# The first weights of a channel mixer split by adding DMAs, and a gate's conditioning moved to the mixer's front

## The chip, the cores and the metric

The kernel runs on one core of one Trainium2 chip. The metric is the device time of one execution in microseconds (us). TensorE (PE in the rows) multiplies, VectorE (DVE), ScalarE (ACT) and GpSimd (POOL) work elementwise, and SyncE (SP) issues most DMAs. Each engine runs its own queue strictly in order.

## The reference

One layer of a streaming encoder, float32, 512 tokens of width 1024, one sequence. A conditioning vector c gives six vectors of width 1024: a shift, a scale and a gate for each of the two sub-layers. The first is a token mixer (attention and a state-space branch, merged and projected). The second is the channel mixer, about which the change is:

```python
c_act = jax.nn.silu(c)
mod = c_act @ w_ada[l] + b_ada[l]
sh_m, sc_m, g_m, sh_f, sc_f, g_f = [m[:, None, :] for m in jnp.split(mod, N_MOD, axis=-1)]
...
x = _layer_norm(DEEPNORM_ALPHA * x + (1.0 + g_m) * y, ln1_g[l], ln1_b[l])
h = _normalize(x) * (1.0 + sc_f) + sh_f
gate, up = jnp.split(h @ w_ffn_in, 2, axis=-1)        # 1024 -> 2 x 2816
y = (jax.nn.silu(gate) * up) @ w_ffn_out              # 2816 -> 1024
x = _layer_norm(DEEPNORM_ALPHA * x + (1.0 + g_f) * y, ln2_g[l], ln2_b[l])
```

`g_f`, the last gate, is wanted only in the last line.

## The kernel before

**Products.** A float32 operand x is split in two rounded parts, `hi` (a copy in the type float32r) and `lo = x - hi`, and a product is three matmuls: hi·hi, hi·lo and lo·hi (`mm3`). So each weight tile costs a load into `raw` (512 KB, 8 buffers), a copy on ACT into `whi` (4 buffers) and a lower part in `wlo` (4 buffers). Before the change the lower part is made in one of two ways. `sub` subtracts on DVE or POOL. With `eng=None` (in `unit`, for the attention's weights) ACT writes -raw rounded, which is -hi, into `wlo`, and POOL issues a DMA that adds `raw` to it: an *adding DMA*.

**Tiles in a pool and slots.** Scratch tiles of 512 columns are 53 slots (`s0` to `s52` in the rows), taken by `get()` and given back by `put()`; the eight PSUM banks are `b0` to `b7`. A buffer is reused only when its last reader is done, so a load into a used buffer waits in SP's queue, and all loads behind it too, since `load` keeps the program's order on SP.

**Order.** A scheduler sets the order of the instructions on each engine from priorities (`prio`). The loads keep the order of the code.

**The stage around the change.** The token mixer ends with the projection `proj` (weights `w_out`), then `ln1_block` runs for each of four blocks of 128 tokens: gate, add, two layer norms, transposes through PSUM (L967), scale and shift (L972, L974), and the split of the modulated activations into the tiles `h0` (high, L978) and `h1` (low, L159 on DVE). The channel mixer then needs both. It begins with four weight units of `w_ffn_in` (two in `raw` buffers as whole units, two in slots by `slot_unit`); `first_half(0)` multiplies them with the first 256 tokens. Two further products for the first two pairs of column tiles, `p_x1` and `p_b`, come next, then `first_half(256)`, and then the loop `for dp in range(ND)` over ten pairs (seven products each, with sums of weights and of activations, which saves multiplications).

**The last gate.** `ada_gate_pe` makes a quarter of g_f: it clears 256 columns on POOL, loads a row of the bias and 8 x 128 x 256 of `w_ada` (two `raw` buffers, called `ra`), multiplies by the conditioning vector on PE (eight narrow matmuls, plain float32, which the trace counts as 16) and adds on DVE (L272). Before, the four quarters stand in the loop at dp 2 to 5. At dp 6 two matmuls with a matrix of ones spread the gate over all partitions (L1168). The tiles are those of the first gate, `gmx`.

Of the kernel before, what the change touches and what calls it, by code (L numbers as in the profile page):

```python
# [17 lines left out]
ALU = mybir.AluOpType  # L18
# [40 lines left out]

ENG, FENG = "VGVVVGVGGGGVVGGG", "GGGV"  # L60

# [20 lines left out]
def _build(tc, I, out):  # L82
# [75 lines left out]
    def sub(dst, a, b, eng=V):  # L158
        return eng.tensor_tensor(dst, a, b, ALU.subtract)  # L159

    def split(x, n=512, eng=V, keep=False):

        h, l = get(F32R), get(F32R)
        acopy(h[:, :n], x[:, :n])  # L164
        sub(l[:, :n], x[:, :n], h[:, :n], eng)
        if not keep:
            put(x)
        return h, l

    def unit(view, a, b, eng=V):  # L170


        with prio("feed"):
            raw = wp.tile([P, D], F32, tag="raw", name=nm("raw"), bufs=NRAW)
            load(raw.rearrange("p (a b) -> p a b", a=a), view)
            hi = wp.tile([P, D], F32R, tag="whi", name=nm("whi"), bufs=NHI)
            lo = wp.tile([P, D], F32R, tag="wlo", name=nm("wlo"), bufs=NHI)
            acopy(hi, raw)  # L178
            if eng is None:
                act(lo, raw, AF.Copy, scale=-1.0)  # L180
                G.dma_start(out=lo, in_=raw, accum_op=ALU.add)
            else:
                sub(lo, raw, hi, eng)
        return hi.rearrange("p (a b) -> p a b", a=a), lo.rearrange("p (a b) -> p a b", a=a)
# [718 lines left out]
    with prio("mix"):  # L903
# [92 lines left out]
        for i in range(NT):  # L996
            with prio("first"):
                ln1_block(i)
        put(*l1g, *l1b)


    with prio("ffn"):
        first, wx = [], []
        for i in range(FIRST):
            for c in (0, FH):
                view = w_f[:, :, c + P * i:c + P * i + P]
                if len(first) < 2:
                    w = unit(view, KC, P, (V, G)[FENG[len(first)] == "G"])
                    w = [[x[:, k, :] for x in w] for k in range(KC)]
                else:  # L1010
                    pair = slot_unit(view, KC, P, (V, G)[FENG[len(first)] == "G"])
                    wx += pair
                    w = [[x[:, k % 4 * P:k % 4 * P + P] for x in pair[k // 4]] for k in range(KC)]
                first.append(w)
# [34 lines left out]

        def operand(x):  # L1050
            with prio("feed"):
                hi = wp.tile([P, D], F32R, tag="whi", name=nm("whi"), bufs=NHI)
                lo = wp.tile([P, D], F32R, tag="wlo", name=nm("wlo"), bufs=NHI)
                acopy(hi, x)  # L1054
                sub(lo, x, hi)
            return hi, lo

        def product(o, x, h, first):
            w = operand(x)
            for q in range(2):  # L1060
# [42 lines left out]
        def p_x1(dp):  # L1103
            d = dps[dp]
            d["a"], d["c"] = piece(dp, 0, 0), None
            d["X"], d["c1"] = bk.get(), get()
            product(d["X"], d["a"], half(0, 0), True)
            acopy(d["c1"], d["X"])

        def p_b(dp):  # L1110
            d = dps[dp]
            d["b"] = piece(dp, 0, 4)
            o = bk.get()
            product(o, d["b"], half(4, 0), True)
            tt(d["c1"], o, d["c1"], ALU.add)
            bk.put(o)
            silu(d["c1"])

        first_half(0)
        for dp in range(2):  # L1120
# [7 lines left out]
        acts, spent = [], []  # L1128
        gfx = gmx
        for g in part:  # L1130
# [3 lines left out]
        for dp in range(ND):  # L1134
# [26 lines left out]
            d["f"] = d["c1"], v  # L1161
            if 2 <= dp < 6:
                j = dp - 2
                ada_gate_pe(5, j, gfx[j // 2][:, j % 2 * 256:j % 2 * 256 + 256])
            if dp == 6:
                for j in range(2):
                    p_ = bk.get()
                    mm(p_, ones, gfx[j], True, True)  # L1168
                    act(gfx[j], p_, AF.Identity, bias=one_c)
                    bk.put(p_)  # L1170
        put(*held)
# [121 lines left out]
```

## Time and profile before

| | us |
|---|---|
| time, median of 3 runs | 824.61 (824.35 to 826.85) |
| profiled execution, its own time | 824.6 |
| its span | 822.9 |
| PE busy in the span | 758.1 (92%) |
| DVE busy | 586.4 (71%) |
| ACT busy | 438.8 (53%) |
| POOL busy | 148.4 (18%) |

The span is the time from the first to the last instruction on the core. A busy share is an average over stages that have different limits, so it is read stage by stage below.

### The profile page before, as it was taken

The page shows a single profiled execution, that of the slowest core. Times are in us where ns is not written, and L with a number is a line of the kernel's source. Part 1 is how long each engine was busy: PE and PEld are TensorE (multiplying, and loading weights), DVE is VectorE, ACT ScalarE, POOL GpSimd, SP SyncE. Part 2 cuts the span into 40 slices and gives each one's busy share as a digit, 9 for nine tenths or more (in the row PEclk, how much of TensorE's full clock was granted, in tenths as well). Part 3 has the DMA queues.
Part 4 walks back from the last instruction along what each step waited for, and adds up shares of the span by engine and source line. Part 5 has one row for each costly group of instructions (what it writes and reads, how often), then busy time and mean ns, then how long its engine had stood idle before and what let it go on. Part 6 is the DMA issues. An engine that isn't in the chain of part 4 may idle for free.

```text
span 822.9 us, 12321 instructions
## 1 busy us (share of the span) xinstructions
PE 758.1 (92%) x4767; PEld 667.5 (81%) x4767; DVE 586.4 (71%) x975; ACT 438.8 (53%) x715; POOL 148.4 (18%) x161
## 2 busy tenths in 40 slices
PE   4989989999996797999994999999999999999995
PEld 2878879988885676787883989999999999888884
DVE  5798474884658774878799898777787876434267
ACT  4375644678987676761435473534445456532211
POOL 1443244512323221001634000000000000000013
PEclk9999998999997999899998899999999999999998
DMA  9992227964207792925941004414445344440001
GB/s 281 361 242 67 52 64 153 237 137 77 52 10 196 228 232 92 350 70 187 358 120 52 1 19 136 155 53 146 144 143 183 104 139 145 157 148 27 1 26 76
DMA packets 99498, 111.49 MB, mean 135 GB/s; under 512 B 4456, under 2 KB 86384, under 8 KB 99440
## 3 DMA queue, kind: packets, MB, share of 16 engines
q1 hardware_dynamic: 95552, 96.82, 37.1%
q0 software_dynamic: 3744, 13.63, 9.0%
q8 instruction: 37, 0.61, 0.3%
q10 hardware_dynamic: 144, 0.26, 0.1%
q14 instruction: 21, 0.17, 0.1%
HBM read 94.97 MB, written 2.10 MB: 118 GB/s over the span
## 4 chain that ended last, share of the span: by engine, by line
PE 75%; DVE 10%; DMA 6%; issue 3%; ACT 2%; SPq 2%; POOL 1%; POOLq 0%; DVEq 0%; ACTq 0%
PE b L149 74%; DMA ra<-w_ada 3%; SPq L146 2%; DMA s<-w_in 1%; DVE s L252 1%; DVE st L288 1%; DMA raw<-w_glu 1%; DMA wlo<-raw 1%; DVE h L159 1%; DVE s L407 1%; DMA s<-x 0%; DVE s L159 0%; DVE s L972 0%; DVE s L943 0%; DVE s L477 0%
## 5 line engine op out<-in xcount | busy, mean ns | idle before, releaser
L149 PE MATMUL b<-h,whi 128*128 128x256 f32 (+1 forms) x896 | 216.5, 331 | 20.8 <-DVE h L159 9.4
L149 PEld LDWEIGHTS b<-h,whi 128*128 128x128 f32 x896 | 151.5, 191 | 36.5 <-DVE h L159 9.6
L159 DVE TENSOR_TENSOR wlo<-raw,whi 128x1024 fp32r<-128x1024 f32 x103 | 129.6, 1264 | 72.1 <-ACT whi L178 37.1
L149 PE MATMUL b<-s,whi 128*128 128x256 f32 (+1 forms) x800 | 168.5, 308 | 7.6 <-ACT whi L178 6.8
L149 PE MATMUL b<-h,wlo 128*128 128x256 f32 (+1 forms) x448 | 148.2, 331 | 1.4 <-DMA wlo<-raw 1.4
L149 PEld LDWEIGHTS b<-s,whi 128*128 128x128 f32 x800 | 129.7, 190 | 18.0 <-ACT whi L178 6.9
L149 PE MATMUL b<-whi,s 128*128 128x512 f32 (+1 forms) x392 | 122.6, 390 | 0.0
L149 PE MATMUL b<-s,wlo 128*128 128x256 f32 (+1 forms) x400 | 121.5, 306 | 0.0
L159 DVE TENSOR_TENSOR s<-s,s 128x512 fp32r<-128x512 f32 (+4 forms) x112 | 76.4, 689 | 56.4 <-PE b L149 23.0
L178 ACT CAST whi<-raw 128x1024 fp32r<-128x1024 f32 x66 | 69.0, 1048 | 84.7 <-PE b L149 66.5
L1054 ACT CAST whi<-raw 128x1024 fp32r<-128x1024 f32 x70 | 72.7, 1050 | 77.5 <-PE b L149 41.6
L149 PEld LDWEIGHTS b<-h,wlo 128*128 128x128 f32 x448 | 85.8, 192 | 8.9 <-DMA wlo<-raw 1.9
L149 PEld LDWEIGHTS b<-whi,s 128*128 128x128 f32 x392 | 73.2, 188 | 16.6
L149 PE MATMUL b<-s,s 128*128 128x128 f32 (+2 forms) x438 | 81.9, 317 | 2.0 <-POOL s L159 1.4
L164 ACT CAST s<-s 128x512 fp32r<-128x512 f32 (+1 forms) x106 | 57.7, 569 | 41.3 <-DMA s<-w_in 12.1
L149 PEld LDWEIGHTS b<-s,wlo 128*128 128x128 f32 x400 | 75.7, 190 | 3.7
L149 PEld LDWEIGHTS b<-s,s 128*128 128x128 f32 x438 | 68.5, 192 | 11.2 <-POOL s L159 1.6
L149 PE MATMUL b<-wlo,s 128*128 128x512 f32 (+1 forms) x196 | 76.4, 390 | 0.0
L1233 POOL TENSOR_TENSOR s<-s,s 128x512 f32<-128x512 f32 x6 | 8.5, 1430 | 357.1 <-DVE s L1232 357.1
L159 POOL TENSOR_TENSOR s<-s,s 128x512 fp32r<-128x512 f32 (+1 forms) x32 | 40.2, 1264 | 79.0 <-ACT s L164 77.6
L1047 DVE TENSOR_TENSOR raw<-raw,raw 128x1024 f32<-128x1024 f32 x40 | 48.6, 1219 | 4.8 <-DMA raw<-w_ffn_in 4.3
L252 DVE SCALAR_TENSOR_TENSOR s<-ra,ca,s 128x256 f32<-128x256 f32 x88 | 47.2, 557 | 4.0 <-DMA ra<-w_ada 3.2
(246 smaller groups left out, 1096.1 us busy)
## 6 DMA issues: line engine op xcount, KB each, us to landing
raw<-w_ffn_in SPq DMA_DIRECT2D x44, 512.0 KB, 4.5
ra<-w_ada SPq DMA_DIRECT2D x32, 512.0 KB, 7.2
raw<-w_in SPq DMA_DIRECT2D x26, 512.0 KB, 4.7
wlo<-raw POOLq DMA_DIRECT2D x26, 512.0 KB, 5.2
raw<-w_ffn_out SPq DMA_DIRECT2D x22, 512.0 KB, 3.3
wa<-w_ada SPq DMA_DIRECT2D x12, 512.0 KB, 7.6
raw<-w_out SPq DMA_DIRECT2D x12, 512.0 KB, 6.5
s<-x SPq DMA_DIRECT2D x16, 256.0 KB, 3.4
```

The source lines that it names most:

```text
L146: return tc.keep_in_program_order(nc.sync.dma_start(out=o, in_=i))
L149: return nc.tensor.matmul(o, lhsT, rhs, start=start, stop=stop, skip_group_check=True, **kw)
L159: return eng.tensor_tensor(dst, a, b, ALU.subtract)
L164: acopy(h[:, :n], x[:, :n])
L178: acopy(hi, raw)
L252: stt(dst, r_, ca[:, k:k + 1], init if k == 0 else dst, ALU.mult, ALU.add)
L288: V.bn_stats(st[:, i, :], x)
L407: e.scalar_tensor_tensor(p_, n, -c, p_, ALU.mult, ALU.add)
L1047: tt(r, x, y, ALU.add)
L1054: acopy(hi, x)
L1233: G.tensor_tensor(z[h], z[h], l2b[h], ALU.add)
```

## The change

`FENG`, which put the lower parts of the four first units on POOL, POOL, POOL and DVE, goes; all four now use adding DMAs (`eng=None`), in slots too. So do the `p_x1` and `p_b` products of dp 0 and 1, which used DVE. The four quarters of the last gate and its two spreading matmuls move from the loop to just ahead of `first_half(0)`, into two slots of their own (`gfx`).

```diff
-ENG, FENG = "VGVVVGVGGGGVVGGG", "GGGV"
+ENG = "VGVVVGVGGGGVVGGG"
...
+    def lower(l, x, h, eng):
+
+        if eng is None:
+            act(l, x, AF.Copy, scale=-1.0)
+            G.dma_start(out=l, in_=x, accum_op=ALU.add)
+        else:
+            sub(l, x, h, eng)
+
     def split(x, n=512, eng=V, keep=False):
 
         h, l = get(F32R), get(F32R)
         acopy(h[:, :n], x[:, :n])
-        sub(l[:, :n], x[:, :n], h[:, :n], eng)
+        lower(l[:, :n], x[:, :n], h[:, :n], eng)
...
-                    w = unit(view, KC, P, (V, G)[FENG[len(first)] == "G"])
+                    w = unit(view, KC, P, None)
...
-                    pair = slot_unit(view, KC, P, (V, G)[FENG[len(first)] == "G"])
+                    pair = slot_unit(view, KC, P, None)
...
-            product(d["X"], d["a"], half(0, 0), True)
+            product(d["X"], d["a"], half(0, 0), True, None if dp < 2 else V)
...
-            product(o, d["b"], half(4, 0), True)
+            product(o, d["b"], half(4, 0), True, None if dp < 2 else V)
...
+        gfx = [get(), get()]
+        for j in range(4):
+            ada_gate_pe(5, j, gfx[j // 2][:, j % 2 * 256:j % 2 * 256 + 256])
+        for j in range(2):
+            p_ = bk.get()
+            mm(p_, ones, gfx[j], True, True)
+            act(gfx[j], p_, AF.Identity, bias=one_c)
+            bk.put(p_)
         first_half(0)
...
-            if 2 <= dp < 6:
-                j = dp - 2
-                ada_gate_pe(5, j, gfx[j // 2][:, j % 2 * 256:j % 2 * 256 + 256])
-            if dp == 6:
-                for j in range(2):
-                    p_ = bk.get()
-                    mm(p_, ones, gfx[j], True, True)
-                    act(gfx[j], p_, AF.Identity, bias=one_c)
-                    bk.put(p_)
```

In the rows of the order below, a number behind a name tells tiles of one name apart, and line numbers of the changed kernel are up to seven away from those before.

PE, where the channel mixer begins, right behind the last matmul of `proj`, before. `s33` and `s52` are the normed second block, `whi_707` and `wlo_708` the first unit, `s30` a part of the third:

```order
L967 MATMUL b3_69<-ident_99,s33_689_4169 128x128 x4
L967 MATMUL b2_68<-ident_99,s52_688_4157 128x128 x4
L149 MATMUL b7_73<-h0_64,whi_707_4285 128x256
L149 MATMUL b0_66<-h0_64,s30_713_4297 128x256
L149 MATMUL b7_73<-h1_65,whi_707_4285 128x256
L149 MATMUL b7_73<-h0_64,wlo_708_4286 128x256
```

The same place in the changed kernel, from the second load of the first quarter on. `ra_...` are the gate's weights, `caz` the conditioning vector, `whi_736`, `wlo_737` and `whi_740` belong to `p_x1` of dp 0 and 1, `s39` and `s42` are the normed third block:

```order
L149 MATMUL b7_73<-ra_727_4333,caz_113 32x256 x4
L149 MATMUL b0_66<-ra_728_4342,caz_113 32x256 x4
L149 MATMUL b0_66<-ra_729_4348,caz_113 32x256 x4
L149 MATMUL b1_67<-s28_724_4323,ones_104 128x512
L149 MATMUL b7_73<-h0_64,whi_736_4492 128x256
L149 MATMUL b7_73<-h1_65,whi_736_4492 128x256
L149 MATMUL b0_66<-h0_64,whi_740_4525 128x256
L149 MATMUL b0_66<-h1_65,whi_740_4525 128x256
L970 MATMUL b4_70<-ident_99,s39_696_4208 128x128 x4
L970 MATMUL b5_71<-ident_99,s42_697_4220 128x128 x4
L149 MATMUL b7_73<-h0_64,wlo_737_4493 128x256
L149 MATMUL b7_73<-h0_64,whi_736_4492 128x256
```

Before, the first products are those of `first_half(0)`; after, half of the gate and then `p_x1`, while `first_half(0)` stands behind `p_x1` of both pairs and `p_b` of dp 0.

SP's loads behind the last of the four first units (`raw_717`), before (724 and 728 are for `p_x1`, 732 and 735 for `p_b`, 766 and 767 for the loop):

```order
L146 DMA raw_717_4305<-w_ffn_in 128x8x128
L146 DMA raw_724_4417<-w_ffn_in 128x4x256
L146 DMA raw_728_4449<-w_ffn_in 128x4x256
L146 DMA raw_732_4481<-w_ffn_in 128x4x256
L146 DMA raw_735_4513<-w_ffn_in 128x4x256
L146 DMA raw_766_4717<-w_ffn_in 128x4x256
L146 DMA raw_767_4719<-w_ffn_in 128x4x256
```

The same queue after, from the second quarter of the gate on (734 and 738 are for `p_x1`, 742 for `p_b`):

```order
L146 DMA ra_728_4342<-w_ada 128x4x256
L146 DMA ra_729_4348<-w_ada 128x4x256
L146 DMA s3_725_4324<-b_ada 1x256
L146 DMA ra_730_4357<-w_ada 128x4x256
L146 DMA ra_731_4363<-w_ada 128x4x256
L146 DMA s3_725_4324<-b_ada 1x256
L146 DMA ra_732_4372<-w_ada 128x4x256
L146 DMA ra_733_4378<-w_ada 128x4x256
L146 DMA raw_734_4489<-w_ffn_in 128x4x256
L146 DMA raw_738_4522<-w_ffn_in 128x4x256
L146 DMA raw_742_4555<-w_ffn_in 128x4x256
```

Eight loads of `w_ada` now stand ahead of the weights of `p_x1`. By the buffers that the two programs give them, `ra_730` takes the buffer of the first unit, `ra_732` that of the second (`raw_709`), `ra_731` and `ra_733` those of `ra_726` and `ra_727`, `raw_734` that of `ra_728`.

POOL at the same place after, behind the last lower part of `w_out` (before, the same stretch has four subtractions for `wlo_708`, `s48`, `wlo_711` and `s21`, and then the clearing of two tiles):

```order
L159 TENSOR_TENSOR wlo_673_3980<-raw_671_3977,whi_672_3979 128x1024
L165 DMA s20_721_4317<-raw_717_4309 128x512
L267 MEMSET s3_725_4324 128x256 x2
L267 MEMSET s28_724_4323 128x256 x2
L165 DMA wlo_708_4286<-raw_706_4283 128x1024
L165 DMA wlo_711_4293<-raw_709_4290 128x1024
L165 DMA s48_714_4300<-raw_712_4297 128x512
L165 DMA s21_716_4305<-raw_712_4297 128x512
L165 DMA s17_719_4312<-raw_717_4309 128x512
L165 DMA wlo_737_4493<-raw_734_4489 128x1024
L165 DMA wlo_741_4526<-raw_738_4522 128x1024
```

The subtractions on POOL are gone and adding DMAs stand in their place, ten in all with the two of `p_b` that follow.

## Rows read from the trace of the kernel before

**Rows 1.** The page: busy time of each engine, and the granted clock in 40 slices.

```profile
PE 758.1 (92%) x4767; PEld 667.5 (81%) x4767; DVE 586.4 (71%) x975; ACT 438.8 (53%) x715; POOL 148.4 (18%) x161
PEclk9999998999997999899998899999999999999998
```

**Rows 2.** Windows: stretch, length, busy us of each engine, granted clock, DMA share, GB/s.

```profile
400.00:430.00 30.00, 30.00 (x133) 24.41 (x132) 24.42 (x30) 6.19 (x13) 16.78 (x7) 1.00 0.68 214
430.00:460.00 30.00, 17.00 (x87) 14.76 (x86) 29.90 (x51) 13.75 (x24) 9.27 (x8) 0.77 0.11 36
460.00:500.00 40.00, 38.21 (x320) 37.53 (x319) 35.41 (x65) 27.89 (x60) 0.00 (x0) 1.00 0.09 27
600.00:700.00 100.00, 100.00 (x803) 96.49 (x802) 76.71 (x82) 53.23 (x70) 0.00 (x0) 1.00 0.43 137
```

**Rows 3.** Chain that ended last, in order of time, from 500 to 812.

```profile
504.55 304.37 PE b L149 x2088
```

**Rows 4.** Timeline of PE, 439 to 478: start, us, what, idle before and its releaser.

```profile
439.79 1.03 PE L967 MATMUL b<-ident,s 128*128 128x128 f32 x8
444.38 0.39 PE L149 MATMUL b<-h,whi 128*128 128x256 f32 x1 [3.56 <-ACT h L978]
454.32 0.58 PE L149 MATMUL b<-h,whi 128*128 128x256 f32 x1 [9.44 <-DVE h L159]
...
475.10 0.50 PE L149 MATMUL b<-h,whi 128*128 128x256 f32 x2 [0.64 <-ACT whi L1054]
476.90 0.66 PE L967 MATMUL b<-ident,s 128*128 128x128 f32 x4 [0.87 <-ACT s L962]
477.85 0.50 PE L149 MATMUL b<-h,whi 128*128 128x256 f32 x2 [0.28 <-ACT whi L1054]
```

**Rows 5.** Windows at PE's restart, columns as in rows 2.

```profile
445.00:454.30 9.30, 0.00 (x0) 0.00 (x0) 9.30 (x17) 1.12 (x3) 1.13 (x4) 0.53 0.00 0
454.30:459.20 4.90, 4.88 (x23) 4.88 (x24) 4.90 (x9) 0.82 (x1) 0.00 (x0) 0.50 0.00 0
```

**Rows 6.** Timeline of PE around one quarter of the gate in the loop.

```profile
549.92 0.28 PE L149 MATMUL b<-h,wlo 128*128 128x256 f32 x1
550.13 1.07 PE L149 MATMUL b<-ra,caz 128*32 128x256 f32 x16
551.13 0.50 PE L149 MATMUL b<-s,whi 128*128 128x256 f32 x2
```

**Rows 7.** Timeline of PE around the two matmuls that spread the gate.

```profile
620.73 1.88 PE L149 MATMUL b<-s,ones 128*128 128x512 f32 x4
622.04 0.80 PE L149 MATMUL b<-s,whi 128*128 128x256 f32 x2
```

**Rows 8.** Timeline of DVE between 439 and 455.

```profile
439.17 2.68 DVE L159 TENSOR_TENSOR h<-s,h 128x512 fp32r<-128x512 f32 x1
441.77 1.75 DVE L948 SCALAR_TENSOR_TENSOR s<-s,s 128x512 f32<-128x512 f32 x1
...
445.84 1.20 DVE L159 TENSOR_TENSOR wlo<-raw,whi 128x1024 fp32r<-128x1024 f32 x1
...
453.58 1.29 DVE L159 TENSOR_TENSOR h<-s,h 128x512 fp32r<-128x512 f32 x2
```

**Rows 9.** Timeline of POOL between 438 and 443.

```profile
438.91 2.39 POOL L159 TENSOR_TENSOR wlo<-raw,whi 128x1024 fp32r<-128x1024 f32 x1 [0.55 <-ACT whi L178]
441.25 1.72 POOL L159 TENSOR_TENSOR s<-raw,s 128x512 fp32r<-128x512 f32 x1
```

**Rows 10.** Timeline of ACT from 437, behind it a pair of the attention (ACT, then POOL).

```profile
437.08 0.81 ACT L962 ACTIVATE s<-s,mv 128x512 f32<-128x512 f32 x1
437.80 1.04 ACT L178 CAST whi<-raw 128x1024 fp32r<-128x1024 f32 x1
...
145.86 1.06 ACT L180 ACTIVATE wlo<-raw 128x1024 fp32r<-128x1024 f32 x1 [4.51 <-PE b L149]
147.22 0.88 POOL L181 DMA_DIRECT2D wlo<-raw  x1 [2.73 <-ACT wlo L180]
```

**Rows 11.** The adding DMAs' line, L181: durations of the issue (min/median/max ns), time to landing.

```profile
L181 POOL DMA_DIRECT2D wlo<-raw x26: 827/869/1057, 50.9 to 303.6; - x26
DMA to landing us min/median/max: 4.5/5.2/8.9
```

**Rows 12.** The tile `raw` from 395 to 480: issues on SP, and time to landing.

```profile
L146 SPq DMA_DIRECT2D raw<-w_ffn_in x10: 367/368/1456, 402.6 to 441.3; - x10
DMA to landing us min/median/max: 3.6/5.6/6.7
```

**Rows 13.** DMA issues from 280 to 310: count, KB each, median us to landing.

```profile
ra<-w_ada SPq DMA_DIRECT2D x6, 512.0 KB, 9.1
wlo<-raw POOLq DMA_DIRECT2D x4, 512.0 KB, 8.3
```

More of the change, by code (lines that the diff above doesn't have):

```diff
@@ L178, in unit @@
             acopy(hi, raw)
[L179 to L183, printed above, removed]
+            lower(lo, raw, hi, eng)
         return hi.rearrange("p (a b) -> p a b", a=a), lo.rearrange("p (a b) -> p a b", a=a)
@@ L998, in _build @@
                 ln1_block(i)
-        put(*l1g, *l1b)
+        put(*l1g, *l1b, *gmx)
     with prio("ffn"):
@@ L1048, in plus, with operand @@
             return r
-        def operand(x):
+        def operand(x, eng=V):
             with prio("feed"):
@@ L1054, in operand, with product @@
                 acopy(hi, x)
-                sub(lo, x, hi)
+                lower(lo, x, hi, eng)
             return hi, lo
-        def product(o, x, h, first):
-            w = operand(x)
+        def product(o, x, h, first, eng=V):
+            w = operand(x, eng)
             for q in range(2):
@@ L1128, in _build @@
         acts, spent = [], []
-        gfx = gmx
         for g in part:
```

## The prediction

> **What bounds the kernel now.** The page first: PE is busy 92% of the span, DVE 71%, ACT 53%, POOL 18% [rows 1]. So PE is the engine to follow, and the change matters where PE waits or where it has less to do. The windows then show where PE is the limit. From 600 to 700 it is busy all 100.00 us with the clock at 1.00; from 430 to 460 it is busy 17.00 of 30 us, with the clock at 0.77, while DVE is busy 29.90 of the 30 [rows 2]. The chain of work that ended last says the same of the loop: one piece of PE, 304.37 us long and beginning at 504.55 [rows 3]. Any PE work that leaves the loop is therefore time saved, and DVE or ACT work that leaves it saves nothing.
>
> The stage between is the layer norm with the start of the channel mixer. PE's timeline has two long waits there: 3.56 us before 444.38 for `h0` from ACT, and 9.44 us before 454.32 for `h1` from DVE. Three short ones follow, 0.64, 0.87 and 0.28 us, for ACT [rows 4]. After 454.32 PE runs without a long wait. The windows add the clock: it falls during the long wait (0.53 on average) and stays at 0.50, which is the level of 1.2 GHz, for 4.90 us of dense work [rows 5]. So every restart after such a wait costs a slow stretch, before and after the change alike.
>
> **What the change removes from the loop.** A quarter of the gate takes PE from 550.04 (the matmul at 549.92 and one regular step of 0.12) to 551.13, so 1.09 us [rows 6]; four are 4.36 us. The two spreading matmuls take from 620.73 to 622.04, 1.31 us [rows 7]. Sum: 5.67 us, all of it in the stretch that PE bounds. The additions on DVE and the loads go too, but nothing waits for them there.
>
> **What it takes off DVE and POOL.** In the stretch before `h1` DVE does lower parts itself, such as the 1.20 us at 445.84. It is also slowed while POOL subtracts: the `h1` subtraction at 439.17 takes 2.68 us, and 1.29 us for two of its kind at 453.58, thus about 0.65 alone; the one at 441.77 takes 1.75 us [rows 8], and POOL's subtractions run at 438.91 and 441.25 [rows 9]. Removing four DVE subtractions, a sum that moves behind and POOL's interference brings `h1` of the second block forward by some 7 us, to about 447. If PE waited for DVE only, this would be the gain. It does not, because of the order.
>
> **What PE waits for instead.** After the change PE's first dense work is `p_x1`, and its third matmul on that unit needs `wlo_737`. The matmuls of `first_half(0)`, whose weights are long in SBUF, are queued behind it, so PE cannot do them meanwhile. The chain to `wlo_737`, step by step:
>
> 1. ACT is free for the -raw of the second first unit at 437.80, where the copy of the same unit stands now, behind the activation at 437.08 [rows 10]. It is done at 438.85 (1.05 us).
> 2. POOL issues the adding DMA 0.30 us after ACT's end (146.92 to 147.22) [rows 10]: 439.15.
> 3. It lands after 5.2 us, the median of 26; bounds 4.5 and 8.9 [rows 11]: 444.35. Only now is the raw buffer free.
> 4. SP, which stood at `ra_732` for that buffer, issues it, `ra_733` and `raw_734`, 0.37 us each [rows 12]: the last at 445.09. `ra_731` and `ra_733` also wait for the gate's matmuls on PE, which run from 439.8 to about 443 in the first wait, so earlier.
> 5. `raw_734` lands after 3.6 to 6.7 us, median 5.6 [rows 12]. It is the third of four issued together, beside adding DMAs; I take 6.7: 451.8.
> 6. Copy and -raw on ACT: 0.95 and 1.06 us, 453.8; POOL 0.30: 454.1; landing 5.2: **459.3**.
>
> Before, PE restarted at 454.32. So the restart is 5.0 us later, although its data from DVE are earlier.
>
> **From the restart to the end.** The matmuls are the same. Added to this busy stretch: the second half of the gate (2 x 1.09 = 2.18 us) and one of the two spreading matmuls (0.66); the other half runs in the first wait and is free. Taken away: the eight transposes of the third block, now done while PE waits (some 0.8 us), and the three short waits of before (1.79). In their place comes a wait for `wlo_744` of `p_b`. Its buffer is that of `wlo_737`, read to the end some 4.7 us after the restart (22 matmuls at the low clock); copy, -raw, POOL and landing add 7.5, so it is there 12.2 us after the restart, and PE, with the second `p_x1`, the gate and the transposes of the last block, comes to it after 11.9: 0.3 us. Sum of the stretch: 2.18 + 0.66 - 0.8 - 1.79 + 0.3 = +0.55. The ten ACT operations for -raw (some 8.6 us) and the second pair of gate additions lie beside PE's waits; DVE's work for the last block and the sums of activations is wanted only after `first_half(256)`, some 12 us of PE work later, and is covered.
>
> **Sum.** +5.0 + 0.55 - 5.67 = -0.1 us. The profiled execution took 824.6 us (span 822.9 and 1.7 around it), the median of the runs is 824.61, so the forecast is 824.5 us. Within 0.3%, about 2.5 us, a measurement of this kernel cannot be told from no change; that is 822.1 to 827.1.
>
> **A rule weighed.** The issue of an adding DMA by POOL takes 827 to 1057 ns in all 26 cases [rows 11], in stretches where DVE was busy, though not at 99.7% as here [rows 2]. The Trainium skill, SBUF — State Buffer (section SBUF: two separate sides), holds that DMAs issued from POOL starve for descriptors while DVE runs an operation in a two-port mode, and gives 620 ns alone against some 3100 ns beside one. By that the three adding DMAs on the chain would each be some 2.5 us later, an estimate from the page that would make it about 832 us; the 26 issues show no such thing so far, and the sum goes by the rows.
>
> **The rivals.** *Faster: the chain is short.* With the lows of the rows (4.5 for adding DMAs, 3.6 for the load) the restart falls to 443.65 + 0.74 + 3.6 + 2.01 + 0.30 + 4.5 = 454.8, and the time to 820.0. Half-way, at 457, it is 822.2, where "faster" begins. For it speaks that most loads have stopped by then: the share of the DMA engines from 430 to 460 is 0.11 [rows 2]. Against it speaks that the change itself puts eight loads and five adding DMAs there.
>
> *Slower: adding DMAs beside loads.* From 280 to 310, with six loads of `ra` under way, the same adding DMA took 8.3 us to land and the loads 9.1 [rows 13]. The chain has three adding DMAs one behind another (for `wlo_711`, `wlo_737` and `wlo_744`), so every microsecond on each counts three times. With 8.3 for all three: 3 x 3.1 = 9.3, thus 833.8. It decides from 6.1 us each (3 x 0.87 = 2.6). For it speaks that `ra_731` to `ra_733` and the slots' adding DMAs run in the same microseconds; against it, that the loads are half as many as there. A POOL issue that waits for a DVE operation of 1.2 us to end, three times, would come to 828 and belongs here.
>
> *No gain in the loop.* If the loop were held by its weights, the 5.67 us would not come back: 830.2. The unbroken 304.37 us of PE speak against it.
>
> **How the numbers follow.** The forecast, restart late and loop shorter by as much: 0.45, with its own range 822 to 827. The short chain: 0.27, of which the far end at 820. The adding DMAs slow: 0.25; no gain in the loop: 0.03. The bounds of all steps together would reach from 819.9 (lows) to 835.6 (8.9 for three adding DMAs); leaving out the far tails gives 820 to 831. Faster 0.27, same 0.45, slower 0.28.
>
> **What would show it.** In PE's timeline after the change: the gate's first matmuls directly behind `proj`; a wait of about 10 us that ends with a DMA of `wlo`, not with DVE, near 459; DVE's `h1` for the second block near 447, so long before it is used; no `ra` matmuls after 500, and the loop's unbroken piece shorter by 5 to 6 us. Right in sign but wrong in size it would be if the restart moved by the landing of `ra_732` or `raw_734`. It would be wrong in its reason if PE's restart were still released by DVE or ACT, or if the first dense work had no wait for `wlo` at all.

## The result, and the profile after

The change makes the kernel **slower by 0.63%**: 829.24 us (median of 15 runs, 824.16 to 832.32) against 824.64 before; ratio 1.0063, 95% interval 1.0046 to 1.0080. Forecast was no change (824.5). The time lies in the range given (820 to 831), but beyond 0.3%, so the likeliest case was not the one that came.

The page of the changed kernel (rows 1 before): busy time of the engines, granted clock, and the queue of the adding DMAs.

```profile
PE 757.7 (92%) x4767; PEld 668.2 (81%) x4767; DVE 575.5 (70%) x969; ACT 446.6 (54%) x725; POOL 148.2 (18%) x167
PEclk9999998999997999899998799999999999999998
q0 software_dynamic: 5184, 17.83, 11.8%
```

PE, DVE and POOL do no more than before; ACT has 7.8 us more. These are averages over the whole span; the windows show where the time goes (columns as in [rows 2]):

```profile
430.00:460.00 30.00, 16.80 (x98) 11.75 (x97) 24.72 (x55) 20.51 (x37) 5.17 (x6) 0.82 0.95 251
460.00:500.00 40.00, 36.33 (x282) 34.31 (x283) 29.10 (x56) 26.20 (x57) 2.63 (x3) 0.88 0.36 81
500.00:600.00 100.00, 100.00 (x848) 100.00 (x848) 77.68 (x80) 47.55 (x60) 0.00 (x0) 1.00 0.37 116
```

From 430 to 460 the DMA engines, nearly idle before (share 0.11), are busy at 0.95, and DVE is no longer full. From 460 to 500 PE's clock is lower than before (0.88 against 1.00). The chain of waits between 440 and 480 of the changed kernel names what is late:

```profile
447.57 8.48 DMA raw<-w_ffn_in
...
456.13 1.04 ACT whi L1057
...
458.66 4.53 DMA wlo<-raw
...
470.72 5.88 DMA wlo<-raw
...
476.65 3.55 PE b L149 x15
```

It names the forecast's links, with a load of 8.48 us instead of 6.7. PE's timeline shows what PE itself waited for:

```profile
440.99 0.64 PE L149 MATMUL b<-ra,caz 128*32 128x256 f32 x8
457.23 0.79 PE L149 MATMUL b<-h,whi 128*128 128x256 f32 x2 [8.68 <-ACT whi L1057]
459.12 0.80 PE L149 MATMUL b<-h,whi 128*128 128x256 f32 x2 [1.10 <-ACT whi L1057]
461.43 1.97 PE L970 MATMUL b<-ident,s 128*128 128x128 f32 x8 [1.51 <-DVE s L967]
463.24 0.58 PE L149 MATMUL b<-h,wlo 128*128 128x256 f32 x1
476.65 0.56 PE L149 MATMUL b<-h,wlo 128*128 128x256 f32 x1 [2.24 <-DMA wlo<-raw]
480.88 2.40 PE L149 MATMUL b<-h,s 128*128 128x256 f32 x19
```

The gate's matmuls stand right behind `proj`. The long wait, 8.68 us, ends with ACT's copy of `p_x1`'s first weights, the next with the copy of the second, and the third, before the transposes, with DVE. Before 463.24 there is no wait: `wlo_737` landed at 463.19 (458.66 and 4.53 us), just when the transposes were done. Dense work begins at 463.24, 22.25 us after `proj` ends, against 14.53 before (439.79 to 454.32 [rows 4]). `h,s` are matmuls of `first_half`: the first such stretch comes at 480.88.

**How the kernels are compared.** Two places are easy to find in every trace: the end of `proj` (439.79 before, 440.99 after) and the first matmul of the loop's products, `s,whi` (495.01 and 506.19; before, two of them stand alone at 486.46). The stretch between them is the *stage*. `proj` itself ended anywhere from 438.07 to 444.78 in the 20 profiles. The profiles differ long before the first changed instruction (PE's wait near 331 ends at 330.77 before and at 332.48 after), and what varies there stays open. So profiles are compared from that point on. The windows of the stage, before and after:

```profile
439.79:495.01 55.22, 40.43 (x316) 39.31 (x314) 52.12 (x90) 31.88 (x69) 4.31 (x6) 0.88 0.07 21
```

```profile
440.99:506.19 65.20, 48.33 (x381) 43.49 (x381) 46.56 (x88) 39.58 (x79) 6.21 (x8) 0.84 0.58 144
```

The stage grew by 9.98 us and the rest, to PE's last matmul (813.13 and 816.18), shrank by 8.13, from 318.12 to 309.99. Forecast were +5.55 and -5.67. With 0.55 more behind PE's end and 1.20 more ahead of the stage that is the 3.6 us between the two profiled executions (824.6 and 828.17). So stage and loop explain 1.85 of the 4.60 us between the medians; 1.75 lie outside them and 1.0 between the medians and the profiled executions, and the cause of these stays open.

### The profile page after: what moved, and what is told of

Same layout as the page of the kernel before. It is cut to its first block, busy times and chain, and to the rows that moved or that the text cites. A ratio compares the mean times of both kernels' runs of the same rounds, so it can differ in the third digit from the quotient of the medians.

```text
span 826.5 us, 12362 instructions
## 1 busy us (share of the span) xinstructions
PE 757.7 (92%) x4767; PEld 668.2 (81%) x4767; DVE 575.5 (70%) x969; ACT 446.6 (54%) x725; POOL 148.2 (18%) x167
## 3 DMA queue, kind: packets, MB, share of 16 engines
q0 software_dynamic: 5184, 17.83, 11.8%
## 4 chain that ended last, share of the span: by engine, by line
PE 72%; DVE 10%; DMA 9%; issue 4%; SPq 2%; ACT 1%; POOL 1%; POOLq 0%; ACTq 0%; DVEq 0%
PE b L149 71%; DMA wlo<-raw 2%; DMA ra<-w_ada 2%; SPq L146 2%; DMA raw<-w_in 2%; DVE s L255 1%; DMA raw<-w_ffn_in 1%; DMA s<-w_in 1%; DMA raw<-w_glu 1%; DVE s L159 1%; DVE st L291 1%; DVE s L410 1%; DMA s<-x 1%; DVE s L477 1%; DVE h L159 0%
## 5 line engine op out<-in xcount | busy, mean ns | idle before, releaser
L149 PEld LDWEIGHTS b<-h,whi 128*128 128x128 f32 x896 | 153.8, 194 | 31.4 <-ACT whi L1057 10.9
L149 PE MATMUL b<-s,whi 128*128 128x256 f32 (+1 forms) x800 | 166.0, 306 | 8.1 <-ACT whi L185 8.1
L159 DVE TENSOR_TENSOR wlo<-raw,whi 128x1024 fp32r<-128x1024 f32 x99 | 125.0, 1267 | 65.1 <-ACT whi L185 41.5
L159 DVE TENSOR_TENSOR s<-s,s 128x512 fp32r<-128x512 f32 (+4 forms) x112 | 76.5, 691 | 56.5 <-ACT s L172 23.5
L165 POOL DMA_DIRECT2D wlo<-raw x32 | 28.0, 874 | 124.2 <-ACT wlo L164 101.2
```

What stands on the lines that cost most here:

```text
L149: return nc.tensor.matmul(o, lhsT, rhs, start=start, stop=stop, skip_group_check=True, **kw)
L165: G.dma_start(out=l, in_=x, accum_op=ALU.add)
```

## The experiments

"Stage" and "loop" are these two stretches in each run's profile (PE busy in the stage from its window); the ratio is to the kernel before in the same round, with its interval. Before's median was 823.47 to 824.64 in the rounds, so times of different rounds compare only to about 1 us; gains and losses below are against before's median of the same round. Stage and loop together against before's 373.34 explain each median's difference from before within -1.1 to +2.9 us.

| run | stage | PE busy in it | loop | time | ratio |
|---|---|---|---|---|---|
| before | 55.22 | 40.43 | 318.12 | 824.64 | |
| change | 65.20 | 48.33 | 309.99 | 829.24 | 1.0063 [1.0046, 1.0080] |
| e1 adding DMAs only | 63.77 | 42.69 | 317.03 | 832.71 | 1.0104 [1.0073, 1.0135] |
| e2 gate only | 61.10 | 48.41 | 309.99 | 820.74 | 0.9965 [0.9948, 0.9983] |
| e3 gate, first units add | 66.39 | 50.49 | 309.99 | 828.99 | 1.0055 [1.0031, 1.0079] |
| e4 all add, gate late | 61.16 | 49.56 | 316.04 | 829.56 | 1.0072 [1.0046, 1.0098] |
| e5 gate, idle adding DMAs | 67.86 | 50.70 | 309.95 | 830.36 | 1.0089 [1.0064, 1.0113] |
| e6 p_x1, p_b add | 59.87 | 43.87 | 316.78 | 828.41 | 1.0057 [1.0042, 1.0072] |
| e7 first units add | 53.43 | 41.01 | 317.12 | 820.15 | 0.9953 [0.9934, 0.9972] |
| e8 gate late | 61.45 | 47.45 | 315.22 | 827.96 | 1.0052 [1.0031, 1.0072] |
| e9 gate, idle negations | 65.28 | 51.12 | 309.94 | 824.74 | 1.0001 [0.9986, 1.0016] |
| e10 slots, all add | 69.85 | 50.05 | 310.42 | 832.82 | 1.0109 [1.0085, 1.0134] |
| e11 slots, first units add | 62.18 | 48.88 | 310.42 | 824.84 | 1.0011 [0.9995, 1.0027] |
| e12 slots, gate only | 64.40 | 49.01 | 310.42 | 826.56 | 1.0026 [1.0008, 1.0043] |
| e13 gate, pairs add | 63.65 | 49.52 | 309.99 | 824.56 | 1.0001 [0.9983, 1.0019] |
| e14 pairs add | 50.60 | 39.90 | 317.81 | 818.56 | 0.9944 [0.9922, 0.9965] |
| e15 split gate, all add | 57.40 | 46.59 | 310.09 | 820.54 | 0.9951 [0.9932, 0.9971] |
| e16 half gate, first add | 58.33 | 44.20 | 314.60 | 824.62 | 1.0012 [0.9996, 1.0029] |
| e17 first_half ahead | 71.30 | 50.65 | 310.50 | 834.88 | 1.0117 [1.0088, 1.0147] |
| e18 split gate, pairs add | 52.64 | 46.11 | 310.54 | 815.14 | 0.9888 [0.9866, 0.9910] |

### The two parts, each alone (e1, e2), and two mixtures (e3, e4)

Theory A: the gate's eight loads, ahead of `p_x1`'s weights, crowd the DMA engines with the adding DMAs. Rivals: the adding DMAs alone, or the loads alone. e1 puts the gate's code back into the loop; e2 gives the lower parts back to DVE and POOL:

```diff
-                    w = unit(view, KC, P, None)
+                    w = unit(view, KC, P, (V, G)["GGGV"[len(first)] == "G"])
...
-            product(d["X"], d["a"], half(0, 0), True, None if dp < 2 else V)
+            product(d["X"], d["a"], half(0, 0), True, V)
```

e3 has the second of these hunks (and its like for `p_b`) only; e4 is the change with the gate's block moved down:

```diff
         for dp in range(2):
             p_b(dp)
+        gfx = [get(), get()]
+        for j in range(4):
+            ada_gate_pe(5, j, gfx[j // 2][:, j % 2 * 256:j % 2 * 256 + 256])
...
         first_half(256)
```

> All eight first lower parts come from adding DMAs, and the gate's conditioning stays in the loop, so that p_x1's four weight loads (SP issues) follow the four first units' loads directly, as in the kernel before. Theory A (what costs the time is the crowd: the gate's eight loads of 512 KB stand ahead of p_x1's weights and share the DMA engines with the adding DMAs): the weights of p_x1 are there before 440 us, the adding DMAs land within about 5 us of their issue long before use, PE restarts at 452 to 455.5 us (before 454.3), and the time is 823 to 826. Rival B (the adding DMAs' landing of 4.5 to 5.9 us costs the time by itself, wherever the loads stand): waits on wlo remain in 460 to 500 us and the time is 828 or more.

> The gate's conditioning goes to the front of the channel mixer as in the change, and the eight first lower parts stay on DVE and GpSimd as before. Theory A (the crowd of loads and adding DMAs): the eight gate loads alone leave the SP issues at some 0.4 us each and raw of p_x1 lands some 6 to 7 us after its issue near 444.5, then 0.95 (copy) and 0.65 (DVE subtraction): restart at 453.5 to 456.5, and with the loop's 5.7 to 8.5 us the time is 816 to 821. Rival C (the gate's loads ahead of p_x1's weights cost the time by themselves): raw lands as late as in the change (456), restart at 458 or later, and the time is 824 or more.

> As the change, but p_x1's and p_b's first lower parts are subtracted on DVE instead of coming from adding DMAs; those of the four first units stay adding DMAs. Theory A: SP is still held until the second first unit's adding DMA has landed (445.1), its issues still take some 2 us and raw lands near 456; then copy and subtraction (1.6) instead of copy, -raw, issue and landing (7.1): restart at 457.5 to 459 instead of 463.2, no wait for wlo at 476: 821 to 824.5. Rival B (it is the adding DMAs of the first units and the loads alone, the landing of the others being hidden): 827 to 830.

> As the change with all adding DMAs, but the gate's conditioning is written behind p_x1 and p_b instead of ahead of first_half(0), so that its eight loads stand behind those of p_x1's and p_b's weights on SP. Theory A: p_x1's weights land before 440, PE restarts at 454 to 457, the gate's matmuls stand between those of p_b and partly wait for their loads (1 to 4 us): 817 to 823. Rival D (the crowd only moves with the gate: the adding DMAs of p_x1 and p_b then meet the gate's loads): waits on wlo or ra of 6 us or more behind the restart, 826 to 830.

Measured: 832.71, 820.74, 828.99 and 829.56. So the gate's move alone is a gain and the adding DMAs alone are a loss: theory A's 823 to 826 for e1 is refuted. Its ranges for e3 and e4 failed too; both times lie in the rivals' ranges. In e3 the first lower part of `p_x1` comes from DVE, so no adding DMA stands at the end of the chain and dense work begins at 457.80; yet its time is that of the change. Counted from the end of `proj`, PE's first matmul on `p_x1` comes at 16.3 us in e3 (457.80) and at 16.2 in the change (457.23): the late load is the same, and taking the last adding DMA off the chain brought nothing (DVE has four subtractions more to do there). In e2 that load is issued 3.17 us behind the end of `proj` and lands 6.9 later, in the change 6.58 and 8.48: 4.99 us in all, where the stages differ by 4.10. Where e1 loses is in DVE's timeline, the first line, and then on PE:

```profile
457.54 1.23 DVE L1050 TENSOR_TENSOR raw<-raw,raw 128x1024 f32<-128x1024 f32 x1 [8.62 <-DMA raw<-w_ffn_in]
458.69 0.69 DVE L159 TENSOR_TENSOR h<-s,h 128x512 fp32r<-128x512 f32 x1
```

```profile
461.16 0.58 PE L149 MATMUL b<-h,whi 128*128 128x256 f32 x1 [8.34 <-DVE h L159]
486.95 0.58 PE L149 MATMUL b<-h,wlo 128*128 128x256 f32 x1 [2.94 <-DMA wlo<-raw]
```

The sum of the loop's first two pieces stands ahead of `h1` in DVE's queue, and one of its loads reuses a `raw` buffer that a first unit's adding DMA holds. SP's waits for adding DMAs into `wlo` there are 19.6 us. It is the forecast's kind of wait, at another engine.

### Which adding DMAs (e6, e7, e13, e14)

From here on the recorded texts weigh two theories: L (lateness: loads wait for buffers that adding DMAs hold, and readers wait for a landing) and O (occupancy: the bytes on the DMA engines, and in e13 ACT's extra work, slow everything). All four are made of the hunks above, with the gate in the loop except in e13: `None` for `p_x1` and `p_b` alone (e6), for the four first units alone (e7), for the third and fourth first unit alone (`slot_unit`, the pairs; e14), and this last with the gate at the front (e13).

> Gate in the loop and first units on DVE and GpSimd as before; only p_x1's and p_b's four first lower parts come from adding DMAs. Theory L: those of p_x1 are there in time (their raw lands before 440), those of p_b can be issued only when PE has left their buffer, so that PE waits 2 to 4 us for their landing, near 480 or 487 (2.9 were seen there with all eight); DVE is rid of four subtractions of 1.2 but then stands idle: 825 to 828. Theory O: no load runs beside these four, so nothing is late: 822 to 824.

> Gate in the loop and p_x1's and p_b's lower parts on DVE as before; only the four first units' lower parts come from adding DMAs. Theory L: the two weight loads of the loop's first pieces reuse raw buffers 706 and 709, which these adding DMAs hold until they have landed (near 446), so that DVE's additions of those pieces, which stand ahead of the second h1, wait for loads landing at 452 to 455, against 8.6 us of such a wait with all eight: restart at 454 to 458, time 824 to 828. Theory O: half of the engine time (11 us), the loads land at 455 or later and the time is 827 or more.

> Gate in the loop; only the third and fourth first unit use adding DMAs, all else as in the kernel before. DVE loses two subtractions of 0.68 ahead of its second h1 and GpSimd two that slow DVE. Theory L: as with all four units (820.2) or a little better, since the loop's first loads wait for no adding DMA: 818 to 821. Rival: the gain came from taking the first two units off GpSimd (2.4 to 2.8 us each, which stretch DVE's h1 to 2.68): 822 to 824.

> As the run with the gate at the front and p_x1's and p_b's lower parts on DVE (829.0), but of the four first units only the third and fourth (the slot pairs) use adding DMAs; the first two stay on GpSimd. No load ahead of p_x1's weights waits for an adding DMA any more; 6 of 12 us of adding DMAs and half of ScalarE's negations are left. Theory L (held buffers in SP's queue): raw of p_x1 issued near 443.5 as with the gate alone, 818 to 822. Theory O (engines' and ScalarE's extra work, in proportion): half of the loss of 8.3 is left, 824 to 826.

Measured: 828.41, 820.15, 818.56, 824.56. Those of `p_x1` and `p_b` cost 4.9. For `p_b` the buffer is free only once PE has left it, so nothing hides the landing; the chain of waits of e6, PE's row, and the window behind it:

```profile
477.04 4.52 DMA wlo<-raw
481.56 0.04 issue
481.60 8.46 PE b L149 x46
```

```profile
481.60 0.58 PE L149 MATMUL b<-h,wlo 128*128 128x256 f32 x1 [1.57 <-DMA wlo<-raw]
```

```profile
481.60:486.60 5.00, 5.00 (x23) 5.00 (x24) 1.29 (x2) 1.85 (x6) 0.00 (x0) 0.50 0.55 105
```

PE's own wait for it is only 1.57 us, but the clock then stands at 0.50 for 5.00 us. Of the 4.65 us by which e6's stage is longer than before's, 3.44 are the same matmuls at a lower clock (0.83 against 0.88) and 1.21 are idle time.

Those of the pairs gain 5.3 (theory L's 818 to 821): two of POOL's subtractions go and two of DVE's, and DVE's `h1` and the operation behind it, 2.68 and 1.75 us before [rows 8], take 0.68 each in e14:

```profile
437.69 0.68 DVE L159 TENSOR_TENSOR h<-s,h 128x512 fp32r<-128x512 f32 x1
438.29 0.68 DVE L951 SCALAR_TENSOR_TENSOR s<-s,s 128x512 f32<-128x512 f32 x1
```

POOL's subtraction of the second first unit still runs beside DVE there, and now it is POOL's that is long, 3.42 us against 2.39 [rows 9], while DVE's operations beside it take 0.67 or 0.68:

```profile
438.38 3.42 POOL L159 TENSOR_TENSOR wlo<-raw,whi 128x1024 fp32r<-128x1024 f32 x1
```

So the two engines do slow each other, and it is not always DVE that pays. e7 beat both theories for it (824 or more). But with the gate at the front these gains vanish: e7 and e2 gain 3.3 and 2.9 alone and lose 5.4 together (e3), and the pairs with the gate (e13) come out where theory O put them.

### Occupied engines, without anyone waiting (e5, e9)

e5 is e2 with the change's negations and as many bytes of adding DMAs beside it, into spare slots that nobody reads; e9 is e5 without the last line.

```diff
             sub(l, x, h, eng)
+            if crowd is not None:
+                n = h.shape[-1]
+                for c in range(0, n, 512):
+                    y = get(F32R)
+                    crowd.append(y)
+                    act(y, x[:, c:c + 512], AF.Copy, scale=-1.0)
+                    G.dma_start(out=y, in_=h[:, c:c + 512], accum_op=ALU.add)
```

> The gate at the front as in the change, the eight first lower parts on DVE and GpSimd as before; beside them ScalarE and eight lots of adding DMAs of the change's size, in 16 of 256 KB, write copies of the lower parts into spare buffers that nobody reads, from the upper part, so that no raw buffer is held by them and nobody waits for their landing. Theory O (occupancy: eight adding DMAs take some 23 us of all 16 DMA engines, the queue's share being 74.1 us before and 97.5 after, and that makes the loads late): raw of p_x1 lands near 456 as in the change, and the time is 826 to 830. Theory L (lateness: the raw buffers are held and the lower parts come only when their adding DMAs have landed): 820 to 823, as with the gate alone (820.7).

> The crowd run without its adding DMAs: gate at the front, first lower parts on DVE and GpSimd, and beside them only ScalarE's 16 negations of 128x512 into spare buffers (some 10 us of ScalarE in all). Theory A (ScalarE's own extra work holds the layer norms' Ln, Exp and scaling, which are behind it in its queue): 826 to 830 as in the crowd run (830.4). Theory O (the DMA engines' occupancy made that run slow): 820 to 823 as with the gate alone.

Measured: 830.36 and 824.74, against 820.74 for e2. Against before in their rounds these are +6.9, +0.8 and -2.9: ACT's negations cost some 3.7 and the adding DMAs some 6.1, although nobody reads what they make. So theory O holds a part for the DMAs, while e9 lies between its two ranges (theory A there is ACT's own work). Neither price is pure: the negations read `raw`, so loads into these buffers wait for ACT (SP waits 9.4 us for one of them in e9), and e5's DMAs hold `whi` buffers (a wait of 1.18 us on ACT).

### The gate's place and its buffers (e8, e10 to e12, e16)

e8 is e4 with e2's lower parts. e16 has quarters 0 and 1 at the front, 2 and 3 in the loop, and e3's lower parts. In e10 (all adding DMAs), e11 (as e3) and e12 (as e2) the gate loads into slots and `p_x1`'s and `p_b`'s loads come first:

```diff
+            if j == 5:
+                xs_ = [get(), get()]
+                for h in range(2):
+                    load(xs_[h].rearrange("p (k n) -> p k n", k=2), w_ada[:, k0 + 2 * h:k0 + 2 * h + 2, col:col + 256])
...
+        early = {(k, dp): piece(dp, 0, k) for k in (0, 4) for dp in range(2)}
         gfx = [get(), get()]
```

> No adding DMAs in the eight first lower parts; the gate's conditioning leaves the loop, but is written behind p_x1 and p_b, so that its loads stand behind their weights. Theory L and theory O alike: restart at 454 to 456 as in the kernel before, the gate's matmuls partly in PE's small gaps near 475 to 480, the loop shorter by 8: 816 to 820. A rival (the gate's loads and matmuls cost there what they cost in the loop): 822 to 825.

> The change with all eight adding DMAs and the gate at the front, but the gate's eight loads go to 16 free 128x512 buffers in halves of 256 KB instead of the raw buffers, and p_x1's and p_b's four loads stand ahead of them on SP. So no load waits for an adding DMA of a first unit, while the DMA engines carry the same bytes. Theory L (lateness by held raw buffers): raw of p_x1 is there before 440, restart at 451 to 456; with p_b's landing still exposed (1.6 to 2.9) and the loop's 8: 818 to 823. Theory O: the crowd is the same, 827 to 830.

> As the run before it, with the adding DMAs in the four first units only and p_x1's and p_b's lower parts on DVE. Theory L: the gains of the first units' adding DMAs (3.3) and of the gate (2.9) now add up, since the loads are uncoupled: 814 to 819. Theory O (both crowd the DMA engines between 430 and 450): 824 to 829 as with both and the raw buffers (829.0).

> No adding DMAs in the first lower parts; gate at the front with its loads in free buffers behind those of p_x1 and p_b. Theory L: p_x1's weights come 8 us earlier than with the gate alone (451.1), but PE's restart there waited for DVE's second h1 (452.6) and the first wlo as well, so that the gain over the gate alone (820.7) is 0 to 2: 818.5 to 821. Theory O: the same bytes at the same times, 820 to 822.

> Adding DMAs in the four first units, p_x1's and p_b's lower parts on DVE, half of the gate (four loads) at the front and half in the loop. Theory O: with four loads of 512 KB fewer beside the adding DMAs the crowd goes, and half of the loop's gain of 8 comes on top: 817 to 822. Theory L: p_x1's two loads still wait for the first two units' adding DMAs (440 and 446), land at 445 and 451 or later, and the time is 822 to 826.

Measured: 827.96, 832.82, 824.84, 826.56, 824.62. e16 fits theory L, e11 theory O; e8, e10 and e12 are beyond all ranges given for them. The misses teach most. In e8 and e4 the gate's matmuls (some 7 us of PE in the stage) meet a busy PE, and the loop waits for its first pieces (it takes 315.22 and 316.04 instead of 310; waits of 2.77 and 3.77 us). In e10 DVE waits once more for a piece behind an adding DMA (9.36 us before 463.59). e12 has none of these adding DMAs to wait for and its weights early, and is yet some 5.5 slower than e2: PE does `p_x1` early and then stands before the next block's transposes:

```profile
466.28 1.97 PE L978 MATMUL b<-ident,s 128*128 128x128 f32 x8 [4.18 <-ACT s L973]
```

while `first_half(0)`, whose weights and `h1` are there, is queued behind them (at 481.00). Early weights alone don't help there; that PE's order is the reason is read from the trace, not tested apart.

### The same bytes in another order (e15, e17, e18)

e15 is the change, all adding DMAs included, with the gate in two halves:

```diff
...
+        gate_half(0)
         first_half(0)
         for dp in range(2):
             p_x1(dp)
+        gate_half(1)
         for dp in range(2):
             p_b(dp)
```

> The change with all eight adding DMAs, but the gate's second half is written between p_x1 and p_b, so that p_x1's first load stands ahead of that half's loads on SP and takes the raw buffer of the first unit, whose adding DMA has landed near 440. Theory L: raw of p_x1's first product lands by 446 to 448 instead of 456, restart at 452 to 456 instead of 463, the end comes 3 to 6 sooner: 823 to 826. Theory O: what p_x1 gains is lost behind it, 828 to 830.

Measured: **820.54**, below both ranges and 8.7 faster than the change (7.9 against before in each round). DMA issues of 430 to 460 (count, KB each, median us to landing), the change first, then e15:

```profile
ra<-w_ada SPq DMA_DIRECT2D x4, 512.0 KB, 7.9
raw<-w_ffn_in SPq DMA_DIRECT2D x4, 512.0 KB, 8.5
wlo<-raw POOLq DMA_DIRECT2D x3, 512.0 KB, 4.6
```

```profile
wlo<-raw POOLq DMA_DIRECT2D x4, 512.0 KB, 6.4
raw<-w_ffn_in SPq DMA_DIRECT2D x4, 512.0 KB, 7.0
ra<-w_ada SPq DMA_DIRECT2D x4, 512.0 KB, 12.6
```

The adding DMAs and the gate's loads are slower than in the change; now it is the gate's second half that comes late, and it is wanted last. The weights come first, and the scheduler has put matmuls of `first_half(0)` ahead of the rest, so PE goes on from 450.43 with no wait above 1 us (the row, and the window of the stage):

```profile
450.43 0.58 PE L149 MATMUL b<-h,s 128*128 128x256 f32 x1 [7.95 <-ACT h L981]
```

```profile
439.39:496.79 57.40, 46.59 (x382) 41.43 (x381) 45.84 (x88) 39.37 (x79) 6.19 (x8) 0.91 0.65 164
```

Several orders moved at once, SP's and PE's, and with them those of ACT and DVE. e17 was to move PE's alone, by an order of issue in `product`; e18 joins e15's split to e14's pairs.

```diff
-                    mm3(o[:, q * 256:q * 256 + 256], ...
+                    with after(ahead[:2] if len(ahead) == 2 else []):
+                        mm3(o[:, q * 256:q * 256 + 256], ...
```

> The change with all eight adding DMAs and SP's order as it is; on PE, first_half(0) is made to stand ahead of p_x1 (an order of issue, no wait between engines), behind all of the gate's matmuls. Theory P (PE's in-order queue: p_x1, whose weights come at 463, stood ahead of first_half(0), whose weights were there and whose h1 came at 448): PE restarts when the gate's last load and h1 are there, 450 to 456 instead of 463, and p_x1's weights are there when it comes to them: 820 to 824. Theory L (the loads' lateness decides wherever PE stands): the wait comes back in front of p_x1 or of its p_b, 827 to 830.

> The split of the gate (second half written between p_x1 and p_b) with adding DMAs in the third and fourth first unit only, p_x1's and p_b's lower parts on DVE, the first two units on GpSimd. If the gains add up (pairs 5.3, the split's 8 in the loop less what its matmuls cost in the front): 813 to 817. Rival: DVE's layer norms set the stage's length, as with the slots (824.8 with first adds): 818 to 822.

Measured: 834.88 and **815.14**, the best kernel here (0.9888, interval 0.9866 to 0.9910). e17 doesn't settle its question: the scheduler put the transposes of the later blocks and the gate's second half ahead of `first_half(0)` too, so PE stood 12.02 us before a transpose (462.92) and began `first_half(0)` at 477.59; its time is beyond both ranges. What that transpose waited for is the same late load, by way of two queues: ACT stands before its copy, a layer norm's small operations stand behind the copy, and DVE waits for these (the first row is ACT's, the second DVE's):

```profile
457.63 1.04 ACT L1060 CAST whi<-raw 128x1024 fp32r<-128x1024 f32 x1 [5.31 <-DMA raw<-w_ffn_in]
462.02 0.30 DVE L296 SCALAR_TENSOR_TENSOR mv<-mv 128x1 f32<-128x1 f32 x2 [5.59 <-ACT mv L295]
```

In e18 PE waits twice, briefly, and has the stage's shortest idle time:

```profile
447.33 0.58 PE L149 MATMUL b<-h,s 128*128 128x256 f32 x1 [2.85 <-ACT h L981]
450.70 2.93 PE L149 MATMUL b<-h,s 128*128 128x256 f32 x12 [2.57 <-DVE h L159]
```

e18 is 5.1 faster than e15 against before in each round: in this order too the adding DMAs of the first two units, of `p_x1` and of `p_b` together still cost time. The split without any adding DMA was not run.

## Why the prediction was wrong

By the profile the restart was forecast at +5.0 and came at +7.7, the rest of the stage at +0.55 and came at +2.3, and the loop at -5.67 and came at -8.13: -0.1 in all against +1.85. The step that failed is the sizing of two links of the chain, SP's issues (step 4) and the landing of `raw_734` (step 5), and of what follows the restart. The loop's surplus hid more than half of that by luck.

**The loop: right in kind, too small.** 8.13 came back instead of 5.67, and the same 309.99 stands in e2, e3 and e13. With the gate still in the loop e1 is 1.09 shorter as well, so the gate itself is worth 7.04; why it is 1.4 more than its rows [rows 6, 7] is open.

**`h1` seven microseconds earlier and unused: right.** It begins at 447.96.

**The chain up to `p_x1`'s load: right in its links, wrong in two sizes.** The -raw began at 438.93, POOL issued at 440.27, and the adding DMA had landed at 445.14 (4.87 us; forecast 5.2). Then step 4 failed: SP's issues, forecast at 0.37 each (a median; the row's highest was 1.46 [rows 12]), took up to 1.9, and `raw_734` was issued 2.43 us after the landing instead of 0.74. And step 5: the load took 8.48 instead of 6.7. From there to the landing of `wlo_737` were 7.14 (forecast 7.5). Together that is +2.8 on the forecast's +5.0; the restart measured +7.7. Both links were priced from stretches in which loads stood nearly alone; here they ran while all DMA engines were full:

```profile
444.50:457.00 12.50, 1.13 (x2) 0.30 (x2) 10.35 (x23) 4.92 (x10) 0.18 (x1) 0.70 1.09 283
```

In e2, with the same loads and without the added DMAs, the load took 6.9 us, close to the forecast's 6.7.

**The chain's end: not what PE waited for.** The forecast named a wait that ends with a DMA of `wlo`, and said that its reason would be wrong if ACT or DVE released PE. They did: the 8.68 us end with ACT's copy and the last 1.51 with DVE, the latter as the transposes of the third block stand ahead of the `wlo` matmul in PE's queue. ACT's copy of `p_x1`'s weights holds ACT's queue, and DVE idles behind it:

```profile
456.13 1.04 ACT L1057 CAST whi<-raw 128x1024 fp32r<-128x1024 f32 x1 [5.98 <-DMA raw<-w_ffn_in]
```

```profile
460.52 0.30 DVE L296 SCALAR_TENSOR_TENSOR mv<-mv 128x1 f32<-128x1 f32 x2 [5.50 <-ACT mv L295]
```

So two ways lead from the late load to 463.24, by `wlo_737` and by ACT's queue, and both end there; the forecast had only the first. Both start at the load, so the two wrong sizes count for either. e3, without the first way, was no faster, though DVE has four subtractions more to do there.

**After the restart: mis-sized.** +0.55 was forecast, +2.3 measured: the wait for `wlo_744` is 2.24 instead of 0.3 (its landing 5.88), and after it the clock fell again, to 0.50 from 477 to 480, which the forecast had not. These two are more than the 1.7 us that are missing; right behind the restart the clock was higher than before (0.68 over 5 us against 0.50), which gives some of it back. ACT's extra operations were put beside PE's waits at no cost; e9 gives them some 3.7 beside the gate at the front, by ACT's queue and by held `raw` buffers together.

**The rivals.** "Slower" came, but not by its mechanism: the adding DMAs on the chain, 512 KB each, landed in 4.5 to 5.9 us, not 8.3, and it was the loads that became slow (the three adding DMAs of 256 KB into slots took 6.6 to 8.0, but PE did not wait for them). The rule that was weighed made no difference: POOL's 32 issues into `wlo` took 850 to 1040 ns, and the one at 440.27, beside which DVE was busy throughout, took 850. The starving that the Trainium skill describes (SBUF — State Buffer, SBUF: two separate sides) is not seen here; whether DVE was in a two-port mode then, no run shows.

**What is shown, and what is open.** That the adding DMAs cause the loss is shown by e1 and e2, and the traces of e2 and the change show how in the stage: `p_x1`'s load is 4.99 us later for a stage longer by 4.10. Full DMA engines have a price of their own (e5), and so has the order: e15, with the same adding DMAs and the same bytes, is faster than before. How much of the load's lateness is the held buffer and how much the full engines is not parted. Whether e15's gain is more SP's order or PE's stays open, as e17 failed to part them.

## What to carry to other kernels

A DMA that does an engine's arithmetic also holds its source buffer until it has landed (SP waited 10.5 us for two of them here): look for the next load into that buffer, what is behind it in the issuing queue, and what in each in-order engine stands behind the consumer of that load. Price a load from a stretch with the DMA engines as full as they will be. Load first what is wanted first, and let the gate, wanted last, wait; here the same transfers in that order were 1% faster.

## What the runs showed of the hardware

With the DMA engines' share at 1.07 to 1.09, SP's issue of a 512 KB load, 0.37 us in the median before [rows 12], took up to 1.88 us in the change and 5.5 in e15. Plain loads landed later than the adding DMAs of their size in the change (8.5 against 4.6), and in e15 those that stood last were the slowest (12.6 against 7.0). The Trainium skill, DMA: Bandwidth & Descriptors (Queues, rings and completion order), says that each DMA engine takes turns between the queues it has work for; that fits loads which slow down beside another queue, though no run here shows the turns themselves.

The added DMAs, eight times 512 KB, raised their queue's time from 9.0% of 822.9 us to 11.8% of 826.5 on 16 engines, 23.5 us or 2.9 each. These are packet times, which overlap when several queues run (the share goes above 1), so they are not pure work.

A short wait can bring PE's clock down to its lower level: it stood at 0.50 for 3.00 us behind a wait of 2.24 us in the change, and for 5.00 us behind one of 1.57 us in e6, which waits of 0.64, 1.80 and 0.28 us preceded.

POOL and DVE subtracting at the same time slow one another, and which one pays changes: DVE 2.68 us for an operation of 0.68 before, POOL 3.42 us for one of 2.39 in e14, with DVE at its 0.68.
